# Fourteen taps of the second chunk's depthwise convolution computed on TensorE around two norms of the first chunk

## Chip, cores and metric

One Trainium2 chip, one of its cores. The metric is the device time of one execution in microseconds (us); for each kernel several executions are timed and the median is given. The profile is of one execution that was recorded by itself, with its own time.

## What is computed

The reference is a two-layer decoder trunk over 1024 positions of 1024 channels, in float32. Only the first half of its first layer matters here:

```python
def conformer_conv(x, norm_g, pw1_w, pw1_b, dw_w, dw_b, ln_g, ln_b, pw2_w, pw2_b):
    a, b = jnp.split(rmsnorm(x, norm_g) @ pw1_w + pw1_b, 2, axis=-1)
    h = a * jax.nn.sigmoid(b)
    h = lax.conv_general_dilated(h, dw_w[:, None, :], (1,), [(CONV_WIDTH - 1, 0)],
        dimension_numbers=('NWC', 'WIO', 'NWC'), feature_group_count=h.shape[-1]) + dw_b
    h = jax.nn.silu(layernorm(h, ln_g, ln_b))
    return h @ pw2_w + pw2_b

h = h + conformer_conv(...)
h = h + swiglu_ffn(h, ffn_norm[0], ffn_w_in[0], ffn_w_out[0])
```

The convolution is per channel, causal, 31 taps wide. After it come a norm over the channels (the "channel norm"), a SiLU, a 1024x1024 product (pw2) and the residual sum; then a root-mean-square norm (the "second norm") and a gated feed-forward block of 2816 hidden channels. Attention, the second feed-forward block and the last norm follow, and are not touched.

## The kernel before

**Tiles.** Channels lie on the 128 partitions, in 8 tiles j = 0 to 7; positions lie along the free axis in two chunks c of 512. A large product is made of three TensorE products per pair of tiles (high part by high part, high by low, low by high), issued by `mm3` (L130 to L149): one step of `mm3` is three products on 512 columns. One weight tile of 1024 rows is 8 steps, 24 products. `wload` (L151) brings a weight tile by DMA, ScalarE makes the high part (`wh`, L162), GpSimd the low part (`wl`, L164), in rings of four. `split` (L177) makes the high part (`yh`, ScalarE, L181) and the low part (`yl`, VectorE, L183) of an activation.

**The convolution of a tile**, `conv_tile` (L333 to L377): the bias and tap 0 go into `zb` on ScalarE (L345), taps 1 to 9 on ScalarE (L359) and are added by GpSimd (L360), taps 10 to 30 on VectorE into a PSUM bank (one L353, twenty L363, 128x512 each); L367 adds both halves into `z`, L375 sums over the tiles. In the first chunk some taps are TensorE products instead: ScalarE writes a 128x128 matrix with the tap's weights on its diagonal (L350), TensorE multiplies the shifted input by it (L351), in full float32. In the second chunk none are (`TAPS[1]` is (10, 0)).

**Order of work.** TensorE's instructions run in the order in which the program issues them. Other engines' instructions are put in order by a planner, by the program's order and its own clock; `mark` and `later` add order edges. The generators `yield` the time that their TensorE work should take; `go(main, time)` draws from `main` for that long, and for each microsecond drawn lets the background generator go on by `rate` microseconds of its own yields (L1257 to L1275). The background of this stage is `background()`: the convolution of the second chunk, tiles in the order 4, 5, 6, 7, 3, 2, 0, 1, and then `layernorm(1)`, which waits 28 us of yields, issues `centre(1)` (one product and 8 subtractions L425 on VectorE, 8 squares, 6 additions) and later the statistics. A tile of the convolution yields 3.3 us after every fifth tap and 2 us at its end.

**The stage around the change** (L1449 to L1476 of `run`): `fill` makes the last four pw1 tiles (3, 2, 0, 1) of the second chunk, 64 steps in all, handed out in pieces to places where TensorE would wait. A pw1 tile writes two banks, `pa` (8 steps) and then `pb` (8 steps). The eight PSUM banks form one pool ("mm"); a new tile takes whichever bank is free in the planner's clock and waits on the chip until the last user of that bank is done.

- `centre(0)`, 4 us of `fill`, then `rstd(0, fill, ...)`: the products of the statistics (L221) are queued in `self.sides` and go out between products of `fill`, and 3 us more of `fill` run beside VectorE's reciprocal square root (L272 to L282) and the diagonal `dg` (L233); the spread (L240) multiplies `dg` by ones.
- `normal(0)`: 8 times z scaled (VectorE, L442), SiLU (ScalarE into a bank, L447), `yh`, `yl`.
- 6 us of `fill` (`LNF`), then the 8 pw2 tiles of the first chunk (L473; the sums `h` are L479), then 2.5 us of `fill`.
- `rstd(0, fill)`: the second norm in the same way, and `ffn_y(0, 0)`: 8 times `h` scaled (VectorE, L292), `yh`, `yl`; three of them use a bank.
- `ffn(0, 0)`: gate and up products tile by tile. From tile 12 on the products are done by a scheme of seven block products (`ffn_gu7`), whose inputs `blocks7` (L303, `blocks` L484) makes on VectorE, ScalarE and GpSimd; two of its four blocks are issued at the end of tile 9 and two at the end of tile 10, ordered behind the tile's last VectorE instruction (L644). That runs L634, then ScalarE's L643, then L644.

Of the kernel before, what the change touches and what calls it, by code (L numbers as in the profile page):

```python
# [1 line left out]

# [18 lines left out]
F32 = mybir.dt.float32  # L21
F32R = mybir.dt.float32r
AF = mybir.ActivationFunctionType
# [6 lines left out]
T = 512  # L30
# [3 lines left out]
CW = 31  # L34
# [11 lines left out]
V_DW = 96  # L46
# [28 lines left out]
TAPS = (10, 2), (10, 0)  # L75
# [3 lines left out]
MM = 0.216  # L79
# [19 lines left out]
PRINT = 0  # L99
AHEAD = 2  # L100
WARM = 4.0
ORDER1 = (4, 5, 6, 7, 3, 2, 0, 1)
YB = 16


class Net:
# [216 lines left out]
    def later(self, ins):  # L323

        last = self.marks.get(ins.ins.engine)
        if last is not None:
            self.tc.add_manual_dep(ins.ins, last, mybir.DependencyInfo(
                mybir.DependencyClass.NoSync, mybir.DependencyReason.DATA))

    def mark(self, ins):  # L330
        self.marks[ins.ins.engine] = ins.ins.name

    def conv_tile(self, c, j):  # L333


        nc = self.nc
        u = self.u[c][j]
        dw = lambda w: self.vec[:, V_DW + j * CW + w:V_DW + j * CW + w + 1]
        n1, n2 = {0: TAPS_FIRST, KT - 1: TAPS_END}.get(j, TAPS[0]) if c == 0 else TAPS[c]
        n2 += n1  # L340
        zb = self.Bp.tile([128, T], F32, name="zb", tag="b")
        z = self.Bp.tile([128, T], F32, name="z", tag="b")
        ps = self.mm_ps()
        later = self.later
        later(nc.scalar.activation(zb, u[:, 0:T], AF.Identity,  # L345
                                   bias=self.vec[:, V_DWB + j:V_DWB + j + 1], scale=dw(0)))
        if n2 > n1:
            for w in range(n1, n2):
                dg = self.tp.tile([128, 128], F32, name="dgw", tag="dgw", bufs=2)
                nc.scalar.activation(dg, self.ident, AF.Copy, scale=dw(w))  # L350
                nc.tensor.matmul(ps, dg, u[:, w:w + T], start=w == n1, stop=w == n2 - 1)  # L351
        else:
            later(nc.vector.tensor_scalar(ps, u[:, n2:n2 + T], dw(n2), None, OP.mult))  # L353
            n2 += 1
        for a in range(max(n1 - 1, CW - n2)):
            w = 1 + a
            if w < n1:
                t = self.tmp("cv")
                later(nc.scalar.activation(t, u[:, w:w + T], AF.Copy, scale=dw(w)))  # L359
                nc.gpsimd.tensor_tensor(zb, zb, t, OP.add)  # L360
            w = n2 + a
            if w < CW:
                later(nc.vector.scalar_tensor_tensor(ps, u[:, w:w + T], dw(w), ps,  # L363
                                                     OP.mult, OP.add))
            if a % 5 == 4:
                yield 3.3
        later(nc.vector.tensor_tensor(z, ps, zb, OP.add))  # L367
        n = len(self.z[c])
        if n == 0:
            self.acc[c] = z  # L370
        else:
            old = self.acc[c]
            if n == 1:
                self.acc[c] = self.cp.tile([128, T], F32, name="acc", tag="acc", bufs=2)
            nc.vector.tensor_tensor(self.acc[c], old, z, OP.add)  # L375
        self.z[c][j] = z
        yield 2.0  # L377
# [879 lines left out]
    def go(self, main, time=1e9):  # L1257


        if main is None:  # L1260
            return False
        while time > 0:
            x = next(main, None)
            if x is None:
                return False
            time -= x
            if self.bg is not None:
                self.owed += x * self.rate
                while self.owed > 0:
                    y = next(self.bg, None)  # L1270
                    if y is None:
                        self.bg = None
                        break
                    self.owed -= y
        return True  # L1275
# [11 lines left out]
    def run(self):  # L1287
# [29 lines left out]
        self.pab, self.endp, self.y7 = {}, None, None  # L1317
        self.phi, self.qd, self.kd, self.vd, self.od, self.raw = {}, {}, {}, {}, {}, {}
        self.hd, self.hd2 = {}, {}
        self.nraw = 0  # L1320
        self.off, self.bg, self.marks, self.sides, self.per = [], None, {}, [], 1

        self.halo = self.tp.tile([128, KT, CW - 1], F32, name="halo", tag="halo", bufs=1)
# [22 lines left out]
        taps = self.vec[:, V_DW:V_POSK]  # L1346
        nc.vector.tensor_scalar(taps, taps, 0.5, None, OP.mult)

        def ffn_y(l, c):
            self.y[c] = self.norm_y(c, V_FN0 if l == 0 else V_FN1, pool=NP[l, c])  # L1350

        def conv(c):
            for j in ORDER1 if c else range(KT):
                while (j if c else min(j + 1, KT - 1)) not in self.u[c]:
                    yield 0.5
                yield from self.conv_tile(c, j)

        def background():
            yield from conv(1)
            yield from self.layernorm(1)  # L1360

        def every(f, r, c, *a):
            for n in r:
                yield from f(c, n, *a)
# [7 lines left out]
        go = self.go  # L1372
# [28 lines left out]
        for k in range(KT):  # L1401
            yh, yl = yr[k]
            for ps, (wh, wl) in zip(self.pab[0], w0):
                for b, (x, y) in enumerate(((wh, yh), (wh, yl), (wl, yh))):
                    nc.tensor.matmul(ps, x[:, k, :], y, start=k + b == 0,
                                     stop=k == KT - 1 and b == 2)
# [6 lines left out]
        self.y[0] = yr  # L1413
        sq1 = self.paired([self.squares(self.h[1][k], self.Bp) for k in range(KT)])
        self.behind(conv(0), RATE0)
        go(g)
        self.pw1_out(0, 1, self.rs[0])
# [3 lines left out]
        go(g)  # L1421
        fill = every(self.pw1_tile, ORDER1[KT - 4:], 1)
        go(fill, 4 * TILE)
        self.rest()
        sq = self.centre(0)
        go(fill, WARM)
        self.per = 2
        self.rstd(0, fill, self.paired(sq))
        self.per = 1
        self.normal(0)  # L1430
        self.behind(background(), RATE1)
        go(fill, LNF)
        go(every(self.pw2_tile, range(KT), 0))
        go(fill, 2.5)
        self.rstd(0, fill)
        ffn_y(0, 0)
        self.mark(self.last)
        self.rate = RATE2
# [165 lines left out]
```

## Time and profile before

| | |
|---|---|
| median of 3 executions | 2569.79 us (2569.06 to 2569.8) |
| the profiled execution, its time | 2576.13 us |
| its span, first to last instruction | 2574.4 us |
| mean granted clock of TensorE | 0.983 of 2.4 GHz |
| busy share: TensorE, VectorE, ScalarE, GpSimd | 97%, 65%, 50%, 56% |

PE is TensorE, DVE VectorE, ACT ScalarE, POOL GpSimd. A float32 product on 512 columns shows as two records (x2), one of the three-part products as one. In a timeline a row gives start, duration, engine, line and, in brackets, how long the engine sat idle before and what ended that. Rows of the chain of work give start, duration and what the chain went through. The records of products overlap, so the distance from start to start says how long one takes.

### The profile page before, as it was taken

Reading aid. Unit: us, or ns where it says so; the run is one execution under the profiler, and the core shown is the slowest. Engines: PE = TensorE matmul, PEld = TensorE weight load, DVE = VectorE, ACT = ScalarE, POOL = GpSimd, SP = SyncE. Lnnn points to the kernel's source line nnn. Section 1 sums busy time; section 2 is a strip of 40 time slices with the busy share of each in tenths; the row PEclk is TensorE's granted clock in tenths of the full one; section 3 lists DMA queues with packets and bytes.
Section 4 is the critical chain, followed back from the end, with each engine's and each line's share of the span. In section 5 each row is a group of like instructions: output and inputs, shape, how many; then the busy total and the mean of one; then the engine's idle time right before and its main releaser. Section 6 shows DMA issues by size and latency. Waiting matters only on the chain.

```text
span 2574.4 us, 37096 instructions
## 1 busy us (share of the span) xinstructions
PE 2505.7 (97%) x13026; PEld 2091.7 (81%) x13026; DVE 1668.0 (65%) x3392; ACT 1290.8 (50%) x2511; POOL 1442.5 (56%) x1151
## 2 busy tenths in 40 slices
PE   8999999999899999999999999999999999899997
PEld 7767788898787888888878788888888878798996
DVE  5986798778654555455548465666666655677775
ACT  6565554434534555555544365655555553344444
POOL 6784899666454554555534353544445534556664
PEclk9998999999999999999999999999999999999999
DMA  4111223232465132222355621213212233233332
GB/s 167 57 41 58 83 90 98 82 99 91 147 202 181 57 101 81 85 87 84 103 179 169 200 76 52 70 59 97 82 45 71 70 135 97 62 119 99 99 97 77
DMA packets 110059, 254.09 MB, mean 99 GB/s; under 512 B 17137, under 2 KB 28720, under 8 KB 109872
## 3 DMA queue, kind: packets, MB, share of 16 engines
q1 hardware_dynamic: 109872, 251.72, 31.7%
q8 instruction: 103, 1.69, 0.3%
q14 instruction: 84, 0.69, 0.1%
HBM read 222.18 MB, written 29.42 MB: 98 GB/s over the span
## 4 chain that ended last, share of the span: by engine, by line
PE 74%; DVE 11%; DMA 5%; issue 3%; POOL 3%; ACT 3%; SPq 0%; POOLq 0%; ACTq 0%; DVEq 0%
PE mm L140 51%; PE po L1103 6%; PE sc L1028 5%; PE pt L1078 5%; PE mm L558 5%; DVE mm L363 3%; DMA wr<-in_fout_dram 1%; POOL wl L164 1%; PE mm L221 1%; DMA wr<-in_fin_dram 1%; ACT wh L162 1%; POOL wl L543 1%; DVE yl L183 1%; DVE yt L292 1%; DVE yt L312 1%
## 5 line engine op out<-in xcount | busy, mean ns | idle before, releaser
L164 POOL TENSOR_TENSOR wl<-wr,wh 128x1024 fp32r<-128x1024 f32 (+2 forms) x388 | 714.7, 1844 | 645.8 <-ACT wh L162 615.0
L140 PE MATMUL mm<-yh,wh 128*128 128x512 f32 x1424 | 592.0, 416 | 6.7 <-DVE yl L183 4.7
L140 PE MATMUL mm<-yl,wh 128*128 128x512 f32 x1424 | 566.0, 397 | 4.4 <-DVE yl L183 3.9
L140 PE MATMUL mm<-yh,wl 128*128 128x512 f32 x1424 | 565.3, 397 | 1.7 <-POOL wl L164 1.7
L162 ACT ACTIVATE wh<-wr 128x1024 fp32r<-128x1024 f32 (+2 forms) x388 | 324.1, 835 | 395.9 <-PE mm L140 212.7
L140 PE MATMUL mm<-gh,wh 128*128 128x512 f32 x1360 | 440.9, 404 | 2.9 <-ACT gh L643 2.3
L1082 DVE TENSOR_TENSOR pl<-pt,ph 128x512 fp32r<-128x512 f32 (+3 forms) x320 | 207.0, 647 | 188.4 <-ACT ph L1081 187.3
L140 PEld LDWEIGHTS mm<-yh,wl 128*128 128x128 f32 x1424 | 270.4, 190 | 63.0 <-POOL wl L164 2.1
L140 PEld LDWEIGHTS mm<-yh,wh 128*128 128x128 f32 x1424 | 271.4, 191 | 60.2 <-issue 15.3
L140 PEld LDWEIGHTS mm<-yl,wh 128*128 128x128 f32 x1424 | 271.8, 191 | 49.8 <-DVE yl L183 6.2
L1081 ACT ACTIVATE ph<-pt 128x512 fp32r<-128x512 f32 (+3 forms) x320 | 179.5, 561 | 221.2 <-PE pt L1078 219.3
L140 PEld LDWEIGHTS mm<-gh,wh 128*128 128x128 f32 x1360 | 243.3, 189 | 50.6 <-issue 3.7
L140 PE MATMUL mm<-gh,wl 128*128 128x512 f32 x680 | 270.2, 397 | 3.8 <-POOL wl L164 3.8
L1052 POOL TENSOR_SCALAR PS<-PS,sm,gates 128x31 f32<-128x31 f32 (+9 forms) x256 | 156.3, 623 | 175.6 <-DVE sm L1049 143.6
L363 DVE SCALAR_TENSOR_TENSOR mm<-u,vec,mm 128x512 f32<-128x512 f32 x309 | 227.6, 752 | 9.8 <-PE mm L351 3.5
L360 POOL TENSOR_TENSOR zb<-zb,cv 128x512 f32<-128x512 f32 x140 | 183.2, 1308 | 23.9 <-ACT zb L345 11.1
L1047 ACT ACTIVATE PS<-PS,mx 128x31 f32<-128x31 f32 (+9 forms) x256 | 140.5, 550 | 93.5 <-DVE mx L1040 92.5
L1052 POOL TENSOR_SCALAR PW<-PW,sm,gates 128x640 f32<-128x640 f32 (+4 forms) x128 | 97.7, 765 | 150.1 <-DVE sm L1049 136.1
L657 DVE TENSOR_TENSOR h<-mm,h 128x512 f32<-128x512 f32 x184 | 124.9, 685 | 76.5 <-PE mm L140 75.9
L140 PEld LDWEIGHTS mm<-gh,wl 128*128 128x128 f32 x680 | 128.0, 188 | 37.1 <-POOL wl L164 6.9
L558 PE MATMUL mm<-y,wh 128*128 128x256 f32 x1008 | 135.2, 287 | 2.2 <-DVE wh L543 1.4
L140 PE MATMUL mm<-yP,wh 128*128 128x512 f32 (+1 forms) x416 | 136.9, 408 | 0.0
(251 smaller groups left out, 4662.0 us busy)
## 6 DMA issues: line engine op xcount, KB each, us to landing
wr<-in_fin_dram SPq DMA_DIRECT2D x176, 512.0 KB, 3.4
wr<-in_fout_dram SPq DMA_DIRECT2D x128, 256.0 KB, 2.7
wr<-in_pw_dram SPq DMA_DIRECT2D x38, 512.0 KB, 3.4
wr<-in_fout_dram SPq DMA_DIRECT2D x64, 192.0 KB, 2.4
wr<-in_wq_dram SPq DMA_DIRECT2D x16, 512.0 KB, 4.2
qd<-q SPq DMA_DIRECT2D x32, 256.0 KB, 2.6
qt<-qd SPq DMA_DIRECT2D x32, 256.0 KB, 2.7
wr<-in_wo_dram SPq DMA_DIRECT2D x16, 512.0 KB, 3.7
```

Source lines behind the costliest of these rows:

```text
L140: nc.tensor.matmul(ps, x[:, a, :], y_, start=start and a + b == 0, stop=stop and a == n - 1 and b == 2)
L162: nc.scalar.activation(wh[:, :kt, :cols], wr[:, :kt, :cols], AF.Copy)
L164: e.tensor_tensor(wl[:, :kt, :cols], wr[:, :kt, :cols], wh[:, :kt, :cols].bitcast(F32), OP.subtract)
L360: nc.gpsimd.tensor_tensor(zb, zb, t, OP.add)
L363: later(nc.vector.scalar_tensor_tensor(ps, u[:, w:w + T], dw(w), ps, OP.mult, OP.add))
L558: nc.tensor.matmul(ps, u[:, a], v, start=a + b == 0, stop=a == n - 1 and b == 2)
L1028: nc.tensor.matmul(ps[:, :k1 - k0], q[:, ql:ql + 128], k[:, key0 + k0:key0 + k1], start=e == 0, stop=e == 1)
L1047: nc.scalar.activation(P[:, p0:p0 + pn], P[:, p0:p0 + pn], AF.Exp, scale=-1.0, bias=mx[:, e:e + 1], accum_out=sm[:, e:e + 1])
L1052: nc.gpsimd.tensor_scalar(P[:, p0:p0 + pn], P[:, p0:p0 + pn], sm[:, e:e + 1], self.gates[:, i, gt:gt + 1], OP.mult, OP.mult)
L1081: nc.scalar.activation(ph[:rows, :width], pt[:rows, :width], AF.Copy)
L1082: nc.vector.tensor_tensor(pl[:rows, :width], pt[:rows, :width], ph[:rows, :width].bitcast(F32), OP.subtract)
L1103: nc.tensor.matmul(po[:, o0:o0 + n], v, got[h][:rows, w0:w0 + n], start=fresh[0], stop=last and h == 1 and e == len(prods) - 1)
```

## The change

Five taps of tile 6 and nine of tile 7 (taps 10 to 14 and 10 to 18) of the second chunk become TensorE products. Their diagonal matrices are made ahead on ScalarE (`diagonals`), their products are issued by a generator `taps`: for tile 6 after the 6 us of `fill` that follow `normal(0)`, for tile 7 chained behind what is left of `fill` in the second norm, whose time before the spread goes from 3.0 to 4.6 us. The sums stay in their PSUM banks (`self.pre`) until `conv_tile` comes to these tiles, which then starts VectorE's taps later; the convolution of tiles 6 and 7 waits until its products are issued.

```diff
+FILL6, FILL7 = 5, 9
...
+    def diagonals(self, j, n):
+
+        n1, d = TAPS[1][0], []
+        for w in range(n1, n1 + n):
+            if (w - n1) % 4 == 0:
+                t = self.Bp.tile([128, T], F32, name="dgs", tag="b")
+            d.append(t[:, (w - n1) % 4 * 128:((w - n1) % 4 + 1) * 128])
+            v = V_DW + j * CW + w
+            self.nc.scalar.activation(d[-1], self.ident, AF.Copy, scale=self.vec[:, v:v + 1])
+        self.diags[j] = d
+
+    def taps(self, j):
+
+        n1, d = TAPS[1][0], self.diags[j]
+        ps = self.mm_ps()
+        for i, x in enumerate(d):
+            self.nc.tensor.matmul(ps, x, self.u[1][j][:, n1 + i:n1 + i + T], start=i == 0,
+                                  stop=i == len(d) - 1)
+            if self.sides:
+                self.sides.pop(0)()
+                if self.sides:
+                    self.sides.pop(0)()
+            if i == len(d) - 1:
+                self.pre[j] = ps, len(d)
+            yield 4 * MM
+
     def conv_tile(self, c, j):
...
+        pre = self.pre.pop(j, None) if c else None
...
-        ps = self.mm_ps()
+        ps = pre[0] if pre else self.mm_ps()
...
-        if n2 > n1:
+        if pre:
+            n2 += pre[1]
+        elif n2 > n1:
...
                 while (j if c else min(j + 1, KT - 1)) not in self.u[c]:
                     yield 0.5
+                while c and j in (6, 7) and j not in self.pre:
+                    yield 0.5
                 yield from self.conv_tile(c, j)
...
         self.normal(0)
+        self.diagonals(6, FILL6)
         self.behind(background(), RATE1)
         go(fill, LNF)
+        go(self.taps(6))
         go(every(self.pw2_tile, range(KT), 0))
+        self.diagonals(7, FILL7)
         go(fill, 2.5)
-        self.rstd(0, fill)
+        fill = chain(fill, self.taps(7))
+        self.rstd(0, fill, time=4.6)
         ffn_y(0, 0)
```

## Rows read from the trace of the kernel before

**Rows 1.** The page's first part: busy time, share and instructions of each engine.

```profile
PE 2505.7 (97%) x13026; PEld 2091.7 (81%) x13026; DVE 1668.0 (65%) x3392; ACT 1290.8 (50%) x2511; POOL 1442.5 (56%) x1151
```

**Rows 2.** Busy time by stretch: stretch, length, engines (instructions), PEclk, DMA share, GB/s.

```profile
236.80:241.60 4.80, 0.15 (x1) 0.00 (x0) 3.27 (x7) 4.80 (x8) 2.36 (x1) 0.78 0.05 10
241.60:246.00 4.40, 4.35 (x10) 3.48 (x11) 3.80 (x7) 4.34 (x8) 0.00 (x0) 0.50 0.29 108
246.00:289.60 43.60, 43.60 (x193) 36.08 (x192) 36.25 (x50) 23.71 (x35) 41.68 (x27) 1.00 0.25 79
...
298.20:307.50 9.30, 7.26 (x13) 4.27 (x14) 7.13 (x12) 4.29 (x7) 4.40 (x4) 0.50 0.17 56
307.50:441.00 133.50, 133.50 (x585) 109.61 (x584) 120.04 (x169) 74.50 (x111) 118.01 (x80) 1.00 0.29 86
```

**Rows 3.** PE's waits from 200 to 495 us: total us, times, longest.

```profile
PE mm L140 <- DVE yl L183: 5.2, 2, 4.7
PE mm L240 <- DVE dg L233: 3.2, 1, 3.2
...
PE mm L558 <- POOL y L504: 0.7, 1, 0.7
```

**Rows 4.** The chain of work that ended last, 225 to 500 us: start, us, what.

```profile
231.29 0.86 PE mm L240 x2
...
241.65 50.96 PE mm L140 x214
...
298.27 2.09 PE mm L240 x2
```

**Rows 5.** PE's timeline at the end of the idle stretch after 236.8 us.

```profile
241.65 0.77 PE L140 MATMUL mm<-yh,wh 128*128 128x512 f32 x1 [4.69 <-DVE yl L183]
```

**Rows 6.** DVE's timeline of the channel norm: the fourth and the eighth low part.

```profile
240.81 0.69 DVE L183 TENSOR_TENSOR yl<-mm,yh 128x512 fp32r<-128x512 f32 x1 [0.60 <-ACT yh L181]
...
245.09 0.69 DVE L183 TENSOR_TENSOR yl<-mm,yh 128x512 fp32r<-128x512 f32 x1 [0.60 <-ACT yh L181]
```

**Rows 7.** Line L350 alone (ns min/median/max), and L363 grouped from 303 to 455 us.

```profile
L350 ACT ACTIVATE dgw<-ident,vec x22: 385/388/402, 15.4 to 188.0; 128x128 f32<-128x128 f32 x22
...
L363 DVE SCALAR_TENSOR_TENSOR mm<-u,vec,mm 128x512 f32<-128x512 f32 x120 | 90.3, 753 | 2.9
```

**Rows 8.** ACT's timeline: two places where it sat idle.

```profile
230.43 1.06 ACT L162 ACTIVATE wh<-wr 128x1024 fp32r<-128x1024 f32 x1 [13.40 <-PE mm L140]
...
301.18 0.60 ACT L181 ACTIVATE yh<-mm 128x512 fp32r<-128x512 f32 x1 [6.16 <-DVE mm L292]
```

**Rows 9.** PE's timeline of the second norm.

```profile
294.00 1.03 PE L221 MATMUL mm<-ones,sl 128*128 128x1 f32 x8
...
301.82 0.80 PE L140 MATMUL mm<-yh,wh 128*128 128x512 f32 x1 [1.48 <-ACT yh L181]
303.10 0.80 PE L140 MATMUL mm<-yl,wh 128*128 128x512 f32 x1 [0.48 <-DVE yl L183]
...
310.16 0.39 PE L140 MATMUL mm<-yl,wh 128*128 128x512 f32 x1
```

**Rows 10.** DVE's timeline of the second norm: diagonal, first scaling, last low part.

```profile
297.54 0.69 DVE L233 TENSOR_TENSOR dg<-ident,mm 128x512 f32<-128x512 f32 x1
300.39 0.76 DVE L292 SCALAR_TENSOR_TENSOR mm<-h,vec,mm 128x512 f32<-128x512 f32 x1 [2.17 <-PE mm L240]
...
309.28 0.69 DVE L183 TENSOR_TENSOR yl<-yt,yh 128x512 fp32r<-128x512 f32 x1
```

**Rows 11.** DVE's timeline: end of feed-forward tile 10, and `centre(1)`.

```profile
471.04 0.69 DVE L634 SCALAR_TENSOR_TENSOR mm<-mm,sg 128x512 f32<-128x512 f32 x1
...
474.61 0.69 DVE L644 TENSOR_TENSOR gh<-mm,gh 128x512 fp32r<-128x512 f32 x1 [1.78 <-ACT gh L643]
...
499.00 4.87 DVE L425 SCALAR_TENSOR_TENSOR z<-mm,z 128x512 f32<-128x512 f32 x8
```

**Rows 12.** PE's timeline in feed-forward tile 12, and the product of `centre(1)`.

```profile
489.25 0.50 PE L558 MATMUL mm<-y,wh 128*128 128x256 f32 x2 [0.70 <-POOL y L504]
...
495.24 1.02 PE L422 MATMUL mm<-acc,ones 128*128 128x512 f32 x2
```

More of the change, by code (lines that the diff above doesn't have):

```diff
@@ L1 @@
 from contextlib import ExitStack
+from itertools import chain
 import concourse.bass as bass
@@ L1319, in run @@
         self.hd, self.hd2 = {}, {}
-        self.nraw = 0
+        self.nraw, self.pre, self.diags = 0, {}, {}
         self.off, self.bg, self.marks, self.sides, self.per = [], None, {}, [], 1
```

## The prediction, made before the changed kernel ran

> **What bounds the kernel now.** I read the page's first part, then busy time by stretch around the change, then TensorE's waits there, then the chain of work and the timelines of single engines. TensorE is busy 97% of the span [rows 1]: a product that is added costs its full time unless it falls into an idle stretch of TensorE. By stretch [rows 2] there are two such places. From 236.8 to 241.6 TensorE does nothing and then runs at half clock until 246; around the second norm it idles again and runs at half clock from 298.2 to 307.5. Elsewhere it is full: 43.6 of 43.6 us under pw2, 133.5 of 133.5 in the feed-forward block, at clock 1.00. In that last stretch VectorE is at 120 of 133.5, the place that loses the fourteen VectorE taps, but TensorE waits there for nobody. The waits [rows 3] name what ended the idle time: `yl` (4.7 us) and the diagonal `dg` (3.2 us).
>
> **Where the first wait really lies.** The first idle stretch ends with a product of L140 that `yl` released [rows 5]. Is it pw2's first product, which needs `yl`, or still a product of `fill`? The chain has 214 products from 241.65 to 292.6 [rows 4]. The eight pw2 tiles are 192, the 2.5 us of `fill` behind them four steps, 12, and one of the next step comes before the first statistics: 205. Nine are left, three steps of `fill`, so after the idle stretch comes the rest of the 6 us of `fill`: the first product into `pb` of the last pw1 tile. Its weights and its input are old; what it can wait for is its PSUM bank, which a SiLU of `normal(0)` held until the fourth `yl` (240.81 + 0.69 = 241.5 us [rows 6]). Only about 245.6 does pw2 start. The eighth `yl` is done at 245.8 [rows 6], and pw2 needs it in its eighth step, seven steps of three products at 0.228 us (133.5 / 585 [rows 2]), 4.8 us, after its start. So pw2 does not wait for the channel norm at all.
>
> **Part 1, five taps of tile 6.** They are issued behind the 6 us of `fill`, that is behind the stalled product, at 245.6 us, where the next products are ready. A float32 product of this size takes 0.86 us at full clock [rows 4]: 5 x 0.86 = 4.3 us, all on the path. Bounds: 4.3 us and, if its bank came late too, another wait like the 4.7; I take **+4.3**. ScalarE makes five diagonals at 0.39 us [rows 7], 1.9 us. It sat idle for 13.4 us before 230.4 [rows 8], which covers them if the planner puts them there. If they land in the chain of SiLUs instead (ScalarE busy 4.80 of 4.80 us [rows 2]), the fourth `yl` and TensorE come up to 1.9 us later. I take 0.
>
> **Part 2, nine taps of tile 7.** Before, the statistics ended at 295.03 (294.00 + 1.03 [rows 9]); 3.2 us later `dg` was done (297.54 + 0.69 [rows 10]), the spread took 2.09 us at half clock [rows 4], and VectorE began to scale at 300.39. By count of steps one step of `fill` is left at the norm (33, 7, 4, 5, 10 and 4 of the 64 are drawn before), so three of the eight statistics go out with it. The other five go two by two behind taps 1 to 3, which puts their end 3 x 0.86 = 2.6 us later, at 297.6; `dg` is done at 300.8. In the meantime 4.6 us of taps are drawn, at 0.864 each: six, the rest. They end at 297.6 + 5.2 = 302.8, 2.0 after `dg`. The spread, now at full clock, takes 0.86: VectorE begins at 303.7, **+3.3**. Does TensorE catch up behind it? From 301.82 to 307.5 it ran at half clock: 11 products (13 records, two of them the spread [rows 2]) in 5.7 us, where 0.228 each and the wait of 0.48 [rows 9] make 3.0; 2.7 us could come back. But the last `yl` was done at 309.97 [rows 10] and its product started at 310.16 [rows 9]: VectorE's scaling set the end of this tile already, and it shifts by the full 3.3. The Trainium skill ("TensorE: Matmul & The Clock Gate", section "Why this matters for your kernels") says that idle gaps between bursts send the clock to half rate and should be avoided; by that alone filling this gap would give the 2.7 us back, and the sum below would be 8.0 instead of 10.7. The trace agrees on the clock (0.50 behind both gaps [rows 2]) but not on the gain, and the row decides. The nine diagonals, 3.5 us, fit into ScalarE's 6.2 us of idle time before 301.2 [rows 8]; 0, or part of 3.5 if they are late. The first five taps of tile 6's VectorE part are now issued inside these taps and can stand ahead of the scaling: 5 x 0.75 = 3.8 us [rows 7] less the 2.9 us that VectorE waits for the spread, so 0 to 0.9; GpSimd's additions for them, 0 to 1.3. I take 0.
>
> **Part 3, what VectorE loses.** One L353 and thirteen L363, 14 x 0.75 = 10.5 us. TensorE waits for none of them between 307.5 and 441 [rows 2], so this is worth 0, at best the 0.7 us that feed-forward tile 12 waits for GpSimd's `y` [rows 3].
>
> **Part 4, the background runs ahead.** The taps let the background move on by 0.5 x 14 x 0.864 = 6.0 us of its yields, and tiles 6 and 7 yield 3 x 3.3 = 9.9 us less. At 0.7 per us of the feed-forward block that is 15.9 / 0.7 = 22.7 us earlier for `centre(1)`. Before, it stood one output tile behind feed-forward tile 12 [rows 12], at 177 us of the block's yields, added up from the code; now it comes at 154.4, and tile 10 ends at 155.5, so one step before its end. There VectorE has L634, L644 and then the last two blocks of `blocks7`, for which TensorE already waits [rows 12]. The eight subtractions, 4.87 us in a row [rows 11], are ready first and older in the program. VectorE idles 1.78 us before L644 [rows 11], which takes part of them: 4.87 - 1.78 = **+3.1** on blocks that have no slack. Bounds: 0 if the planner puts them behind the blocks; 6.7 with the six additions at about 0.6 as well, and some 2.4 more if a wait of that length halves the clock as it did at 298. No DMA is added or moved; GpSimd has the same additions, only sooner. Two more banks are held from the taps to `conv_tile`; eight cover four for two feed-forward tiles, two for the convolution and these; if not, a wait like the 4.7 us.
>
> **Sum.** 4.3 + 3.3 + 3.1 = 10.7 us. The profiled span of 2574.4 would become 2585.1. That execution took 2576.1, 6.3 above the median of the runs, and I put the difference on the median: 2569.8 + 10.7 = **2580.5**.
>
> **Rivals.**
> - *The planner keeps `centre(1)` off the blocks.* For it: VectorE has no convolution left there, and the planner's clock is not the chip's. Against: program order. Then 7.6 us, 2577.4.
> - *TensorE catches up behind the second norm*, because its clock no longer falls. For it: half clock there before [rows 2]. Against: the last `yl` [rows 9, 10]. Then 10.7 - 2.7 = 8.0 us, 2577.8. It is the skill's rule above.
> - *The change does what it says: the first wait moves to where the taps stand.* This decides whether the kernel is slower at all. If the stalled `pb` product got a bank that the first `yl` frees, before 236.8, the three steps would run at once and at full clock (2.1 us), the taps from 238.9 to 243.2 and pw2's first tile, 24 products, to 248.6 instead of 251.1: -2.5 where I have +4.3. The term is nought where the bank comes early enough to win 4.3 us, from the second `yl` or sooner. For it: the pool of banks is handed out anew. Against: up to that product the order of allocations is the old one, and only diagonals are new. Then -2.5 + 3.3 + 3.1 = 3.9 us, 2573.7, no change; with the 2.7 us of the rival above, 2571.0.
> - *GpSimd becomes late.* It is busy 118 of 133.5 us [rows 2], and tiles 6 and 7 now hand it the same additions in 14 us less. If weight tiles come late by that backlog, some 6 us on top: 16.7, 2586.5. Against: the rings of four let weights run ahead.
>
> **How the numbers follow.** A measurement of this kernel can tell about 0.2%, 5.1 us, from no change. Chances: my forecast 0.35, the blocks undisturbed 0.22, TensorE catching up 0.08, the wait moved 0.20, GpSimd late 0.05, and 0.10 for a plan that comes out faster elsewhere. All but the wait moved and the last are slower, less 0.05 for their lower ends: slower 0.65. Same is 0.23 (0.20, that 0.05, less 0.02 if the blocks lose their wait too), faster 0.12. The range goes from 2567 (the wait moved and TensorE catching up, less the 3.1 and the 0.7 us of the blocks: 2569.8 - 2.6) to 2588 (4.3 + 3.3 + 2.2 + 6.7 + 1.9 = 18.4). Forecast and first two rivals alone span 2577 to 2584.
>
> **What would show it.** Right: in the timeline the idle 4.7 us stand before three steps of `fill` and the five taps behind them; the spread starts about 4.5 us later after the start of the last statistics than before, at full clock; no wait of TensorE vanishes from 307 to 441; L425 stands ahead of L634 and TensorE's wait for L504 grows from 0.7 to about 4. Wrong: the taps stand in the idle stretch, or pw2 waits for `yl`; L425 behind L504; or an interval of the ratio that reaches 1.

## The result, and the profile of the changed kernel

The changed kernel took 2593.86 us (median of 5, 2591.67 to 2596.0) against 2569.79 for the kernel before on the same chip (median of 5): a ratio of 1.0099 (95% interval 1.0088 to 1.011), 24 us slower. The forecast was 2580.5, slower by 10.7, with a range to 2588: the direction was right, the size less than half. The profiled execution has a span of 2594.3 us (2596.0 with what lies around it), 19.9 us more than that of before.

Lines of the changed kernel are 2 higher than in before up to L331, and 31 higher from the taps of `conv_tile` on (L183 is L185, L292 is L294, L363 is L394, L425 is L456, L504 is L535, L644 is L675); the new taps are L351. The page's first part, which answers to [rows 1]: TensorE is busy 13.7 us longer with 28 more records, VectorE 12.5 us shorter.

```profile
PE 2519.4 (97%) x13054; PEld 2097.8 (81%) x13054; DVE 1655.5 (64%) x3378; ACT 1294.1 (50%) x2525; POOL 1441.9 (56%) x1151
```

TensorE's waits from 200 to 530 us (total us, times, longest), which answer to [rows 3]:

```profile
PE mm L142 <- DVE yl L185: 7.0, 4, 4.7
PE mm L589 <- ACT y L534: 5.1, 2, 3.8
...
PE mm L589 <- DVE y L535: 1.3, 2, 1.1
PE mm L142 <- DVE gh L675: 0.6, 1, 0.6
```

The 4.7 us in front of the `pb` product are still there, and the 3.2 us for `dg` have gone; the other waits for `yl`, at the second norm, have grown from 0.5 us to 2.3. TensorE waits four times for the blocks (L534, L535), 6.4 us in all, where before waited twice, 0.7 us [rows 3] and 0.4. The chain of work around the two norms, against [rows 4]:

```profile
241.50 4.18 PE mm L142 x9
245.68 4.90 PE mm L351 x10
250.57 46.49 PE mm L142 x205
...
298.08 0.97 PE mm L351 x2
...
301.77 5.26 PE mm L351 x12
307.04 0.87 PE mm L242 x2
```

Nine products of `fill` follow the wait, then the five taps of tile 6 (ten records, two for each), then pw2. At the second norm the taps of tile 7 go on until 307.0, and the spread takes 0.87. VectorE there, against [rows 10]:

```profile
304.28 0.68 DVE L235 TENSOR_TENSOR dg<-ident,mm 128x512 f32<-128x512 f32 x1
...
307.93 0.76 DVE L294 SCALAR_TENSOR_TENSOR mm<-h,vec,mm 128x512 f32<-128x512 f32 x1 [0.23 <-PE mm L242]
...
309.91 0.75 DVE L394 SCALAR_TENSOR_TENSOR mm<-u,vec,mm 128x512 f32<-128x512 f32 x1
...
311.83 0.75 DVE L394 SCALAR_TENSOR_TENSOR mm<-u,vec,mm 128x512 f32<-128x512 f32 x1
...
318.63 1.22 DVE L185 TENSOR_TENSOR yl<-yt,yh 128x512 fp32r<-128x512 f32 x1 [0.59 <-ACT yh L183]
```

The first scaling starts at 307.93 instead of 300.39. Two taps of the convolution (L394) stand between the scalings, and the last `yl` waits for ScalarE. Last, the end of feed-forward tile 10 on VectorE, against [rows 11], and tile 12 on TensorE, against [rows 12]:

```profile
482.13 4.86 DVE L456 SCALAR_TENSOR_TENSOR z<-mm,z 128x512 f32<-128x512 f32 x8
...
489.42 0.69 DVE L675 TENSOR_TENSOR gh<-mm,gh 128x512 fp32r<-128x512 f32 x1 [0.62 <-ACT gh L674]
490.03 3.50 DVE L201 TENSOR_TENSOR acc<-acc,sq 128x512 f32<-128x512 f32 x2
...
503.94 0.69 DVE L535 TENSOR_TENSOR y<-et,y 128x512 fp32r<-128x512 f32 x1
```

```profile
500.12 0.58 PE L589 MATMUL mm<-y,wl 128*128 128x256 f32 x1 [3.78 <-ACT y L534]
501.80 0.79 PE L589 MATMUL mm<-y,wl 128*128 128x256 f32 x2 [1.09 <-DVE y L535]
503.87 0.58 PE L589 MATMUL mm<-y,wl 128*128 128x256 f32 x1 [1.28 <-ACT y L534]
```

`centre(1)`'s eight subtractions stand ahead of tile 10's last instruction, its additions (L201) mostly between that and the end of the last two blocks. TensorE waits, and the granted clock of the 20 us from 500 on is 0.76; around the second norm's scalings it is 0.86 where [rows 2] have 0.50 (columns as in [rows 2]):

```profile
307.90:320.00 12.10, 8.10 (x23) 4.91 (x23) 11.48 (x17) 7.17 (x12) 9.88 (x8) 0.86 0.00 0
500.00:520.00 20.00, 17.27 (x93) 15.43 (x94) 10.85 (x19) 7.21 (x14) 10.35 (x9) 0.76 0.28 87
```

**Where the time went.** The table is worked out from the timelines: each moment is counted from the start of the first spread (231.13 us in before), and the same moment of the kernel before is taken off, so +7.7 means 7.7 us late. It holds the runs of the next section too. The block is the first feed-forward block; its parts are groups of tiles with their output sums, and a part ends where its last sum starts on VectorE (L657). The first spread is that of the channel norm, and the third is that of the norm behind the block (695.99 in before); the one of `layernorm(1)` between them is not counted.

| kernel | first scaling | last `yl` | block's part 1 ends | part with tile 12 ends | third spread |
|---|---|---|---|---|---|
| before, once more | 0.0 | 0.0 | 0.0 | -0.1 | -0.2 |
| after | +7.7 | +10.0 | +9.6 | +20.3 | +20.6 |
| `e1_centre_back` | +7.4 | +9.7 | +9.3 | +11.0 | +3.2 |
| `e2_centre_early` | -0.2 | -0.2 | -0.3 | +8.2 | +0.4 |
| `e3_tile6_only` | +4.3 | +4.8 | +3.6 | +4.9 | +3.4 |
| `e4_tile7_only` | +5.7 | +6.7 | +6.1 | +7.2 | -0.7 |
| `e5_two_silus` | -0.1 | -0.1 | -0.2 | -0.2 | -7.3 |
| `e6_four_silus` | +0.6 | +0.6 | +0.6 | +0.6 | -7.1 |
| `e7_after_four_silus` | +8.1 | +10.4 | +10.0 | +12.0 | +5.9 |
| `e8_hold_tile6` | +7.3 | +8.4 | +14.7 | +16.4 | +16.9 |
| `e9_taps_at_spread` | +2.5 | +3.5 | +8.5 | +10.2 | +7.5 |
| `e10_stats_first` | +0.7 | +1.2 | +7.8 | +8.9 | +9.9 |
| `e11_after_29` | +7.4 | +9.8 | +9.4 | +16.8 | +10.5 |

The changed kernel loses 10 us at the two norms and about 10 around tile 12, and keeps both. Two profiles of before agree within 0.2 us at each of these moments; behind the third spread, which the change does not touch, they differ by 6.4 us (from the first spread to the end 2343.3 and 2336.7).

### The profile page after: what moved, and what is told of

The parts are those of the page before. It is cut to its first block, busy times and chain, and to the rows that moved or that the text cites. A ratio compares the mean times of both kernels' runs of the same rounds, so it can differ in the third digit from the quotient of the medians.

```text
span 2594.3 us, 37148 instructions
## 1 busy us (share of the span) xinstructions
PE 2519.4 (97%) x13054; PEld 2097.8 (81%) x13054; DVE 1655.5 (64%) x3378; ACT 1294.1 (50%) x2525; POOL 1441.9 (56%) x1151
## 4 chain that ended last, share of the span: by engine, by line
PE 76%; DVE 11%; DMA 4%; POOL 3%; issue 3%; ACT 3%; SPq 0%; POOLq 0%; ACTq 0%; DVEq 0%
PE mm L142 54%; PE po L1134 6%; PE sc L1059 5%; PE pt L1109 5%; PE mm L589 4%; DVE mm L394 3%; DMA wr<-in_fin_dram 1%; DMA wr<-in_fout_dram 1%; POOL wl L166 1%; POOL wl L574 1%; PE mm L223 1%; ACT wh L164 1%; DVE wh L574 1%; DVE yl L185 1%; DVE yt L314 1%
## 5 line engine op out<-in xcount | busy, mean ns | idle before, releaser
L394 DVE SCALAR_TENSOR_TENSOR mm<-u,vec,mm 128x512 f32<-128x512 f32 x297 | 216.7, 751 | 10.2 <-PE mm L382 4.8
```

## The experiments

**1. `centre(1)` set back.** The changed kernel with one number changed, so that `centre(1)` stands behind tile 12 as in before.

```diff
-        yield 28.0
+        yield 43.9
```

> The changed kernel with one number different: layernorm(1) waits 43.9 us of background yields before centre(1) instead of 28.0, which by the sum of the yields puts centre(1) back to where it stood in the kernel before (177 us into the feed-forward block instead of 154.4). Theory A (of the 19.9 us between the two profiled spans about 8.5 come from centre(1) landing on the last two blocks of blocks7): this kernel is about 8 us faster than the changed one and 11 us slower than the kernel before, ratio near 1.004, and TensorE waits about 1 us for the products of tile 12 instead of about 6. Theory B (the two PSUM banks held and the shifted convolution cost the time in tile 12): nothing comes back, 19 to 24 us slower than before.

Measured: 2575.83 us, ratio 1.0016 (1.0005 to 1.0027) against the kernel before on its chip (2570.74, also for the next three). Some 19 of the 24 us come back by moving `centre(1)`, more than theory A has (its 1.004 lies outside the interval). The table shows that these are two gains: 9.3 us by the end of the part with tile 12, where the wait for the blocks has gone, and 8 more between there and the third spread. Neither the prediction nor theory A knew of the second.

**2. `centre(1)` moved up in the kernel before.** No taps; `centre(1)` comes as early as in after.

```diff
-        yield 28.0
+        yield 12.1
```

> The kernel before with one number different: layernorm(1) waits 12.1 us of background yields instead of 28.0, so that centre(1) comes 22.7 us of the feed-forward block's yields sooner, one step before the end of tile 10, as in the changed kernel; no taps on TensorE. Theory A: 8 to 9 us slower than the kernel before (ratio 1.0033), with TensorE waiting 5 us or more for the last two blocks in tile 12. Theory B: within 2 us of the kernel before.

Measured: 2572.87 us, ratio 1.0006 (0.9997 to 1.0015). Theory A's total did not come, but its waits did. From 460 to 540 us TensorE has the very ones of after:

```profile
PE mm L558 <- ACT y L503: 5.1, 2, 3.8
PE mm L558 <- DVE y L504: 1.3, 2, 1.1
```

The part with tile 12 ends 8.2 us late, so the place of `centre(1)` alone costs this much. Yet the whole is no slower, because the stretch up to the third spread is 8 us shorter, as in the first experiment.

**3 and 4. The taps of one tile alone.** The changed kernel without the diagonals and taps of tile 7, or of tile 6, with `centre(1)` behind tile 12.

```diff
-        yield 28.0
+        yield 33.5
...
-                while c and j in (6, 7) and j not in self.pre:
+                while c and j == 6 and j not in self.pre:
...
-        self.diagonals(7, FILL7)
...
-        fill = chain(fill, self.taps(7))
-        self.rstd(0, fill, time=4.6)
+        self.rstd(0, fill)
```

> Only the five taps of tile 6, and layernorm(1) waiting 33.5 us so that centre(1) stands where it did before. If the taps stand behind the stalled product and are pure work of TensorE: 4.3 to 4.9 us slower than the kernel before (ratio 1.0018), the idle 4.7 us before the last three steps of fill unchanged. If they fill a wait: no slower, and the idle stretch shorter by as much.

```diff
-        yield 28.0
+        yield 38.5
...
-                while c and j in (6, 7) and j not in self.pre:
+                while c and j == 7 and j not in self.pre:
...
-        self.diagonals(6, FILL6)
...
-        go(self.taps(6))
```

> Only the nine taps of tile 7, and layernorm(1) waiting 38.5 us so that centre(1) stands where it did before. If the taps delay the statistics and then the spread, and the scaling on VectorE sets the end of the next tile: 3.3 us slower than the kernel before (ratio 1.0013). If the clock that stays up gives its time back behind the norm: 0.6 us slower, no difference that can be measured. If the tile that VectorE scales last is late because of the taps of tile 6 only, and not of tile 7, the last low part follows the first scaling by 9.6 us, as before, and not by 11.9.

Measured: 2576.69 us, 1.0023 (1.0014 to 1.0032), with tile 6; 2573.35, 1.001 (1.0002 to 1.0019), with tile 7. At the last `yl` they stand 4.8 and 6.7 us behind before, 11.5 together where after has 10.0: with tile 7 alone TensorE waits 2.3 us for GpSimd's `acc` ahead of the statistics, which tile 6's delay covers in after. The last low part ends 10.6 us after the first scaling there, neither the expected 9.6 nor after's 11.9: VectorE's taps are not between the scalings, but ScalarE's `cv` still are. By the third spread tile 7's kernel has made up 8 us, tile 6's has not.

**5. The order at the end of the block.** In GpSimd's program the kernels that make up those 8 us have one thing in common that the others lack: the last two 128x384 `wl` of the block stand ahead of the second `yl` of `normal(1)`. The kernel before comes to that order by another edit, two SiLUs of `normal(0)` in SBUF instead of PSUM.

```diff
-            s = self.tmp("si") if c or j in LNP[c] else self.mm_ps()
+            s = self.tmp("si") if c or j in LNP[c] or j in (0, 1) else self.mm_ps()
```

> The kernel before, with the first two SiLUs of normal(0) written to SBUF instead of a PSUM bank. By the program the stalled pb product still gets a bank that the fourth yl frees, so the 4.7 us of idle time before it should stay; what changes is the order that comes out at the end of the first feed-forward block, where GpSimd's last two wl of pw2(1) now stand ahead of the second yl of normal(1), as in the kernels whose stretch from the last gl to the third spread took 30 us instead of 37. Theory (that order alone is worth about 7 us): 7 us faster than before, ratio 0.9970 to 0.9978, idle time at the first norm 4.7 us, no change up to the last outs of the block. Rival (the 7 us in the other runs came from something else, such as where centre(1) stands): within 2 us of before.

Measured: 2564.18 us, ratio 0.9972 (0.9961 to 0.9983) against 2571.11 for the kernel before on its chip: with the sixth the fastest kernel of this study, faster than before and after. GpSimd in the second profile of before, and then in this kernel:

```profile
669.72 1.66 POOL L183 TENSOR_TENSOR yl<-si,yh 128x512 fp32r<-128x512 f32 x1 [1.25 <-ACT yh L181]
672.31 1.01 POOL L164 TENSOR_TENSOR wl<-wr,wh 128x384 fp32r<-128x384 f32 x1 [0.93 <-ACT wh L162]
673.28 1.75 POOL L183 TENSOR_TENSOR yl<-si,yh 128x512 fp32r<-128x512 f32 x1
```

```profile
666.66 1.48 POOL L164 TENSOR_TENSOR wl<-wr,wh 128x384 fp32r<-128x384 f32 x1 [1.15 <-ACT wh L162]
668.11 1.29 POOL L183 TENSOR_TENSOR yl<-si,yh 128x512 fp32r<-128x512 f32 x1
```

and TensorE's statistics and third spread, in the same two:

```profile
685.87 0.38 PE L221 MATMUL mm<-ones,acc 128*128 128x1 f32 x2 [3.19 <-DVE acc L199]
...
690.86 0.42 PE L221 MATMUL mm<-ones,sl 128*128 128x1 f32 x2
696.25 1.02 PE L240 MATMUL mm<-dg,ones 128*128 128x512 f32 x2
```

```profile
678.74 0.28 PE L221 MATMUL mm<-ones,acc 128*128 128x1 f32 x2
...
682.68 0.28 PE L221 MATMUL mm<-ones,sl 128*128 128x1 f32 x2
686.55 1.02 PE L240 MATMUL mm<-dg,ones 128*128 128x512 f32 x2
```

Counted from the first spread, the block's last weights are done 2.6 us sooner, the wait of 3.19 us for `acc` is gone, the statistics take 3.9 us from their first start to their last instead of 5.0, and the spread follows 3.9 us later instead of 5.4. This kernel has no taps, so the 7 us do not need them. They belong to an order that the planner chose anew in each kernel: experiments 1, 2, 4 to 7 and 11 have the earlier one, and gain 6 to 8 us between the end of the part with tile 12 and the third spread; before, after and experiments 3, 8, 9 and 10 have a later one, with the last `wl` behind the second `yl` or, in after and 8, behind the third, and gain at most 2.7. That the order comes with the 7 us is shown; which of its shifted instructions makes them was not tried.

**6 and 7. The bank of the `pb` product.** The first four SiLUs of `normal(0)` in SBUF, in the kernel before and in the first experiment's. By the program the `pb` product then has a bank that no SiLU held.

```diff
-            s = self.tmp("si") if c or j in LNP[c] else self.mm_ps()
+            s = self.tmp("si") if c or j in LNP[c] or j in (0, 1, 2, 3) else self.mm_ps()
```

> The kernel before, with the first four SiLUs of normal(0) in SBUF. Now the pb product gets a bank that no SiLU held. Theory: the three fill steps run at once behind the spread, pw2 starts some 4 to 6 us sooner and waits in its first tile for the yl (the eighth is done about 245.8 in the profile of before), so its first tile ends at about 247 instead of 251.1: 4 us gained there, and with the order of the run with two SiLUs 11 us in all against before, ratio about 0.9957; against the run with two SiLUs 4 us. Rival (TensorE merely waits elsewhere, for the same yl, and runs at half clock after it): no more than 1 us against the run with two SiLUs.

> The kernel after, with centre(1) set back behind tile 12 as in the first experiment (2575.8 us) and the first four SiLUs in SBUF. The pb product is free, but the bank of tile 6's taps is the one that the fifth yl frees. Theory (the bank sets where this stretch goes on): the taps wait about as long as the pb product did, to about the fifth yl, and pw2's start moves from 250.6 to about 247.5: 3 us faster than the first experiment, about 2572.8. Rival (the taps cost their 4.8 us wherever they stand): as the first experiment, 2575.8.

Measured: 2564.22 us, 0.9974 (0.9965 to 0.9983), the same as the fifth; and 2574.57, 1.0018 (1.0009 to 1.0028), the same as the first. Both rivals hold. The `pb` steps do run at once, and the wait stands one place further on, first in the kernel before, where pw2's first product has it, then in after, where the taps have it:

```profile
243.24 0.80 PE L140 MATMUL mm<-yh,wh 128*128 128x512 f32 x1 [4.59 <-DVE yl L183]
```

```profile
243.74 7.53 PE L351 MATMUL mm<-u,dgs 128*128 128x512 f32 x10 [4.59 <-DVE yl L185]
```

Behind it TensorE runs at half clock again: the five taps take 7.0 us to the next product (250.71). A free bank for one product only passes the wait to the next one that needs a bank.

**8. Tile 6's convolution held** until the second norm's scalings are issued, `centre(1)` behind tile 12, the later order at the end of the block.

```diff
-        yield 28.0
+        yield 42.0
...
-        self.nraw, self.pre, self.diags = 0, {}, {}
+        self.nraw, self.pre, self.diags, self.shut = 0, {}, {}, True
...
-                while c and j in (6, 7) and j not in self.pre:
+                while c and (j in (6, 7) and j not in self.pre or j == 6 and self.shut):
...
+        self.shut = False
         self.rate = RATE2
```

> The kernel after, with the convolution of tile 6 held until the scalings of the second norm are issued, and centre(1) set back behind tile 12 (one wait of the layer norm 42.0 instead of 28.0). The order at the end of the block stays that of after (the last wl behind all three yl). Theory: without the two taps between VectorE's scalings the last yl comes 2.2 us sooner than in after, so the first feed-forward tile ends 7.5 us later than in before instead of 9.7; no loss in tile 12; the end of the block as in before. So 7.5 us slower than before in all, ratio 1.0029, some 2.4 us slower than the first experiment, which has the better order. Rival (the order at the end of the block is worth nothing and centre(1) alone took the 18 us): 2 us faster than the first experiment.

Measured: 2589.99 us, 1.0077 (1.0065 to 1.009): neither. The last `yl` came only 1.6 us sooner than in after: it ends 10.6 us after the first scaling, where after has 11.9 and before 9.6, so the two taps between the scalings cost 1.3 us. The other 1.0 goes, by the trace, to ScalarE's `cv`, which still stand ahead of the last two `yh`. The held convolution then stood in front of the feed-forward tiles:

```profile
343.49 8.66 DVE L394 SCALAR_TENSOR_TENSOR mm<-u,vec,mm 128x512 f32<-128x512 f32 x11
```

```profile
PE mm L142 <- ACT gh L674: 4.6, 1, 4.6
```

Part 1 of the block ends 14.7 us late, 5 more than in after; from there to the third spread 2 more are lost and none made up, as the later order lets one expect.

**9. Tile 6's taps right behind the first spread,** with their diagonals ahead of the statistics, so that they have a bank before the SiLUs take it; `centre(1)` behind tile 12.

```diff
-        self.rstd(0, fill, self.paired(sq))
+        sq = self.paired(sq)
+        self.diagonals(6, FILL6)
+        self.rstd(0, fill, sq)
         self.per = 1
+        go(self.taps(6))
         self.normal(0)
```

> The kernel after, with the five taps of tile 6 drawn right behind the first spread, ahead of normal(0), and their diagonals ahead of that norm's statistics; centre(1) set back behind tile 12. By the program the taps now have a bank that no SiLU held, seven fill steps follow them, and the pb product behind these waits for the fifth yl, about 242.7 us. The order at the end of the block is that of the kernel before. Theory (taps cost nothing while TensorE would wait anyway): TensorE's idle time there falls from 4.7 to about 1 us, pw2 starts no later than in before (245.6) instead of 4.9 later, the taps of tile 7 keep their delay of 2 to 3 us at the second spread, and the whole is 2 to 4 us slower than before, ratio 1.001. Rival (fourteen products of nearly 1 us cost their time wherever they stand): 9 us slower than before, ratio 1.0035.

Measured: 2581.6 us, 1.0047 (1.0034 to 1.006). At the norm the theory holds, and beyond what it said: TensorE is never idle there, at full clock, where before had 0.15 of 4.80 us busy and then the clock at 0.50 [rows 2]:

```profile
236.00:246.00 10.00, 9.97 (x45) 7.88 (x44) 7.83 (x13) 9.84 (x17) 3.50 (x2) 1.00 0.14 40
```

pw2 starts 2.1 us sooner than in before (its first product at 241.91, 12.35 us behind the first spread, against 14.49), and the last `yl` is only 3.5 us late. But 5 more are lost by the end of part 1, so the total is no better than the rival's, for another reason.

**10. The statistics first.** As the ninth, and tile 7's taps drawn when all statistics are out, five ahead of the spread and four behind it.

```diff
         ps = self.mm_ps()
+        while self.sides:
+            self.sides.pop(0)()
         for i, x in enumerate(d):
...
-        self.rstd(0, fill, time=4.6)
+        self.rstd(0, fill, time=2.6)
```

> The kernel of the run with the taps at the spread, and the taps of tile 7 drawn only when all eight statistics of the second norm are out; five of them ahead of the spread, four behind it, in VectorE's first scalings. Theory: the second spread is at most 1 us later than in before, VectorE's first scaling too, the last yl moves with it, and the kernel is 0 to 2 us from before, ratio 1.000, some 2 us faster than the run with the taps at the spread. Rival (the statistics do not matter, the products do): no difference to that run.

Measured: 2578.81 us, 1.0038 (1.0023 to 1.0053), not to be told from the ninth. Yet all fourteen taps now cost 0.7 us at the first scaling and 1.2 at the last `yl`. At the end of part 1 there are 7.8. The trace of that place, ScalarE, GpSimd and TensorE:

```profile
363.85 0.60 ACT L660 ACTIVATE sg<-mm 128x512 f32<-128x512 f32 x1 [0.62 <-POOL zb L393]
...
361.20 8.03 POOL L393 TENSOR_TENSOR zb<-zb,cv 128x512 f32<-128x512 f32 x6
...
366.33 0.79 PE L142 MATMUL mm<-gh,wh 128*128 128x512 f32 x1 [4.86 <-ACT gh L676]
```

The convolution runs ahead by what TensorE did of it. ScalarE's copies `cv` for GpSimd's additions stand ahead of the gate's SiLU `sg`, and GpSimd works off six additions in 8.03 us; ScalarE waits for a buffer (`cv` and `sg` come out of one ring, `tmp`), `sg` is late, `gh` is late, TensorE waits 4.86 us. This was read from the trace; no run takes it away.

**11. The collision and the order apart.** The changed kernel with the earlier order and `centre(1)` still ahead of tile 12.

```diff
-        yield 28.0
+        yield 29.0
```

> The kernel after with one wait of the layer norm 29.0 instead of 28.0: centre(1) comes six products of TensorE later, still before feed-forward tile 12, and the order at the end of the block becomes the better one. Theory (collision with the blocks about 9 us, order at the block's end about 7, separate): the delay after tile 12 stays 18 to 20 us, and 7 are given back at the end of the block: about 2587, ratio 1.0065. Rival 1 (the order is worth nothing where the rest is late): as after, ratio 1.0099. Rival 2 (six products are enough to let VectorE do the blocks first, by the program its subtractions stand one instruction later and its additions behind the blocks): the delay after tile 12 falls to 11 to 13 us and the ratio to about 1.0025, as in the first experiment.

Measured: 2584.62 us, 1.0056 (1.0042 to 1.007). The part with tile 12 ends 16.8 us late, of which 6.3 are made up by the third spread. The theory's 1.0065 lies inside the interval, both rivals outside. The delay is 3.5 us less than in after; in the trace five of the six additions now stand behind the blocks, and the subtractions with one addition still hold TensorE up there:

```profile
PE mm L589 <- DVE y L535: 3.2, 1, 3.2
PE mm L589 <- ACT y L534: 0.6, 1, 0.6
```

**12. The kernel before once more.**

> The kernel before once more, for a second profile of it: the stretches up to the end of the first feed-forward block should agree within 1 us with the first profile of it, and what differs by execution should lie behind it.

Measured: 2570.54 us, 1.0002 (0.9991 to 1.0013); what its profile shows is in the table and below it.

## Why the prediction was wrong

**The sum.** Forecast 10.7; up to the third spread 20.6 were measured. 7.7 of it are there at the first scaling (forecast 7.6), 2.3 more at the last `yl` (0), 1.2 more up to the last output sum ahead of tile 12 (0), of which a wait for `gh` is 0.6 (459.22 less 230.99 is 228.2 us after the first spread, against 448.14 less 231.13, 217.0: 11.2 late), 9.1 around tile 12 (3.1), and 0.3 behind it. Behind the third spread the two profiled executions differ by only 0.6 (19.9 in all). The medians' 24 is 3.4 more than the 20.6; two executions of one kernel differ by 6.4 behind the third spread, and the 3.4 stay open.

**Part 1 was right.** The taps did fall behind the stalled product, and pw2 came 4.5 us late (its first product at 250.01, 19.0 us behind the first spread, against 14.5 in before) where the forecast had 4.3; the third experiment gives 4.3 to 4.8 for this part alone. The reading of the bank wait held, too. But the rival "the first wait moves" priced the taps with an early bank for `pb` at -2.5 in place of +4.3, and no gain came of such a bank: in experiment 7 the first scaling is 8.1 us late, in the first 7.4. The next product that needs a bank waits instead. The place that does pay is right behind the spread (experiment 9).

**Part 2 was right up to the first scaling and wrong behind it.** 3.2 us (7.7 less 4.5) against 3.3, the spread at 0.87. The sentence that failed is "0 to 0.9; GpSimd's additions for them, 0 to 1.3. I take 0". It bounded taps that stand ahead of the first scaling. Three did stand there and cost nothing; two more stood between the scalings, with ScalarE's `cv` ahead of the last `yh`, and these cost 2.3 (1.3 and 1.0 by experiment 8). TensorE did not catch up, as forecast: its clock there rose from 0.50 to 0.86, and the last `yl` still set the end. The Trainium skill's rule against idle gaps ("TensorE: Matmul & The Clock Gate", section "Why this matters for your kernels") did not decide here. At the first norm it agrees with experiment 9, where the gap was filled, the clock stayed at 1.00 and pw2 started sooner, because there TensorE's own work came next.

**Part 3 was right.** Before has no wait of TensorE from 305 to 470 us that could vanish, and its 1.1 us in tile 12 stayed where the collision was taken away (experiments 1, 3, 4 and 8 to 10).

**Part 4 is the step that failed.** The place was right to one step: `centre(1)` came before the end of tile 10. The price was not. "4.87 - 1.78 = +3.1" let the subtractions use VectorE's idle 1.78 us, and left out the additions and the clock. On TensorE, from tile 12's first product to the first one behind the tile, before and after (columns as in [rows 2]):

```profile
480.59:492.46 11.87, 10.81 (x86) 10.21 (x84) 8.35 (x10) 4.77 (x10) 9.82 (x8) 1.00 0.21 63
```

```profile
492.59:512.91 20.32, 13.93 (x85) 12.84 (x84) 14.03 (x20) 6.80 (x12) 11.18 (x10) 0.75 0.16 53
```

The tile takes 8.4 us longer: 5.3 are waits (6.4 instead of 1.1), and 3.1 are the same products at a granted clock of 0.75 instead of 1.00. The remaining 0.7 of the 9.1 lie around the tile and were not followed up. The waits come from VectorE. There tile 10's last instruction comes at 489.42. In before it came at 474.61 [rows 11]; with the 11.2 us of delay by then and the 0.1 by which the first spread came sooner that would be 485.7, so the subtractions took 3.7. From its end to the end of the blocks' last `y` it now takes 14.5 us (490.1 to 504.6) where before took 10.1 (475.3 to 485.4): the additions among the blocks, and a weight's `wh` that came ahead of them, took 4.4. So the blocks were some 8 us late on VectorE, and the forecast had 3.1. The bounds in the text, 6.7 and 2.4 for the clock, hold the measured 9.1, but the forecast chose near the wrong end, and the range's upper end took the 6.7 without the 2.4. Experiments 1, 2 and 11 bear this out: 9.3 back without the collision, 8.2 with it alone, 3.5 less with most additions behind the blocks.

**What was in no part.** An order at the far end of the block, more than 350 us behind the taps, comes with 7 us (experiment 5), and 7 of the 11 variants have it the other way round than before. It did not add to the loss here, since before and after both have a later order (0.3 us between them); it hid the loss in experiments 2 and 4 and added to the gain in the first, and without experiment 5 the collision would have been put at 18 us.

**GpSimd late** had 0.05. As a wait for weights it did not come. It came as a wait for `gh` in experiments 9 and 10 (3.5 and 4.9 us), whose norms took less time; in after that wait is 0.6 us. The 4.6 us of experiment 8 have VectorE's held taps ahead of them as well.

## What to carry to other kernels

A wait for a buffer belongs to the next instruction that needs one; work fills the idle time only if it stands ahead of the wait and has its own buffer, as the taps behind the first spread did. Work taken from an engine that nobody waits for gives no time back, and it lets what follows on that engine run ahead: look where that lands, and price the landing with everything it brings along, not with its first group of instructions. Where a planner orders the engines, give each part its own run and compare at landmarks, since an edit can also move several microseconds in a place it never touched.

## What the runs showed beyond that

What five products of float32 by float32, 512 columns each, cost by what TensorE did before them: right behind other work (experiment 9), behind the nine products that follow the wait of 4.7 us (the changed kernel), and directly behind a wait of 4.59 us (experiment 7), to the next product each time:

```profile
230.42:234.31 3.89, 3.89 (x11) 1.73 (x10) 2.86 (x5) 2.46 (x5) 1.98 (x1) 1.00 0.23 58
```

```profile
245.47:250.01 4.54, 4.54 (x12) 2.02 (x10) 4.36 (x7) 4.41 (x8) 3.50 (x3) 0.86 0.00 0
```

```profile
243.74:250.70 6.96, 6.96 (x10) 2.92 (x11) 6.17 (x10) 6.90 (x12) 3.03 (x3) 0.57 0.00 0
```

They take 3.9 us at a granted clock of 1.00, 4.5 at 0.86, and 7.0 at 0.57. (The product behind them takes 0.4 us more than its like in all three, so at full clock it is 0.86 us for each, as [rows 4] have it.) The products that stand first behind a gap pay for the clock: in the changed kernel the nine of `fill` do, which take 4.0 us from 241.50 to 245.47 at a granted clock of 0.50 where 0.228 us each would make 2.1.
